# A two-block transformer layer on one core: the planner's price of TensorE's products is changed

## The chip, the cores and the metric

One core of one Trainium2 chip runs the whole program in one launch. The metric is device time in microseconds (us): the median of the timed executions is 954.91 us (three runs, 953.92 to 955.23). Smaller is better.

## The reference, cut to what matters

256 tokens of 1024 features pass through two blocks, all in float32:

```
x = x + gated_branch_mixer(rmsnorm(x))          # w_in (6144 columns), a 31-tap convolution, pooling, w_o
x = x + cross_attention(rmsnorm(x), rmsnorm(mem))
x = x + mixture_of_experts(rmsnorm(x))          # 16 experts, 2 of them for each token
x = rmsnorm(x)                                  # second block:
x = x + rmsnorm(attention_and_scan(rmsnorm(x) @ w_in_2) @ w_out_2)
x = x + rmsnorm(cross_attention_2(rmsnorm(x), rmsnorm(mem_2)))
x = x + rmsnorm(conv_ffn(rmsnorm(x)))           # w_up_2, three-tap convolution, silu * value, w_down_2
```

Every `@ w` is a product with a weight matrix that is read once from the chip's memory, some 178 MB in all.

## The kernel before, in words

**Weights.** All weight matrices lie in one stream, cut into some 330 pieces, nearly all of 512 KB (128 partitions x 1024 floats), in the order of their use. A piece is loaded by SyncE into a tile `stg`. ScalarE (ACT) casts it to `whi`, a float32r tile of fewer bits; VectorE (DVE) writes the remainder `wlo = stg - whi`. An activation is likewise held as two parts, so one block of a weight product is three TensorE (PE) products: whi by the activation's high part, whi by its low part, wlo by its high part. There are six `stg` tiles, four `whi` and three `wlo`, so the splits can be at most two to three pieces ahead of PE.

**Two kinds of work.** A *main line* issues the weight products in the order of the stream (`lin`, `lin_tok`, `lin_both`, `down`, `up_mm`; all products go through `mm`, line 659). Everything else is a *task*: a Python generator that issues a few instructions and yields (class `Task`). Tasks empty PSUM banks, run the norms, the convolution, softmax, routing and the gated scans (`hgrn`, line 1954), and they too issue some products and transposes.

**What sets the order.** All instructions are issued by the Python program once, when the kernel is written, and each engine then runs its own in exactly that order; the order is fixed by hand-written planning and nothing on the chip revises it. The planner keeps a timetable (class `Clock`, line 174): for each engine the time at which it becomes free, and for each tile the time at which its last writer and readers end. `Clock.issue` adds an instruction: it starts when its engine is free and its operands are there, and lasts as long as a price given by the caller. DVE's and ACT's prices are in `Engine.call` (lines 249 to 264), PE's in `mm` (line 662) and in `transpose` (0.107 us, line 666). `now` (line 382) is the time at which the timetable has PE free.

The timetable is read in these places:

- `runnable` (line 420): a task's step that begins with a product may be issued once its operands are there at `now`; another step may be issued if its engine could start it by `now + AHEAD`. AHEAD is 0.8 to 2.6 us by stage (`PACE`, line 281).
- `splits` (line 431): the split of piece n is *due* at `now` plus the sum of `cost(x)` over the pieces from the current one to n (lines 479 to 482). It is put off while its end, by the timetable, lies more than a margin before that. The margin is 0.3 us in a first look and then, after a look at the tasks, 0.5 to 4.0 us by stage (1.0 in the first mixer, 2.0 for the experts, 4.0 in the second mixer, 1.5 in the last stage).
- `block` and `need` (lines 540 and 646): while the main line waits for an activation, due times are moved out by GRACE = 2.0 us.
- `advance` (line 520) ties these together, and is called after every block of weight products until nothing more is due or runnable.

So the prices change no instruction and no operand; they decide how many task steps and splits stand between one weight product and the next, and at which product of the main line a task's own product is put. The prices before are:

```
return nk * nc / 1024 * (1.3 if name.startswith("w_e") else 2.7)
self.c.issue("pe", max(0.107 if slow else 0.027, 0.0022 + n * (4 if slow else 1) / 2400.0), [lhsT, rhs], [out])
```

`n` is the number of columns streamed; `slow` is a float32 product (in norms, attention scores, scans, routing), as against the float32r products of the weights.

Of the kernel before, what the change touches and what calls it, by code (L numbers as in the profile page):

```python
# [35 lines left out]
def weight_plan():  # L36
    """The weight loads in the order of their use: (name, expert, rows, columns)."""
    plan = []
# [87 lines left out]
class Act:  # L126
    """An activation as two float32r parts, with the tasks that write its blocks."""
# [11 lines left out]
class Group:  # L139
    """Two PSUM banks as [128, 4, 256]."""  # L140
# [12 lines left out]
class Task:  # L153
    """A generator that issues instructions; it yields where others may go first."""
# [6 lines left out]
    def at(self):  # L161
        """When its next step can start; None while it waits for others to be issued."""
        t = 0.0 if self.on is None else self.on()
        return None if t is None or self.busy else max(self.ready, t)
# [9 lines left out]
class Clock:  # L174
    """A rough timetable of the engines, kept as the instructions are issued: it decides their order only."""
# [53 lines left out]
class Engine:  # L229
    """An engine whose instructions are entered in the timetable."""  # L230
# [40 lines left out]
class Net:  # L271
# [6 lines left out]
    GRACE = 2.0  # how much later the splits are due while the main line waits for an activation, in us  # L278
    NEAR = 0.5
    # how far the tasks run ahead of the main line, and the slack of the weights' splits, in us  # L280
# [40 lines left out]
    def tile(self, pool, shape, dt, tag, bufs):  # L321
        """A tile of a tag, entered in the timetable as free when the slot's last tile is."""
        t = pool.tile(shape, dt, tag=tag, name=self.name(tag), bufs=bufs)
        name, ring = t.tensor.name, self.rings.setdefault((id(pool), tag), [])
        if len(ring) >= bufs:
            busy = self.busy() if tag == "b" else {x.tensor.name for x in self.kept.get(tag, {}).values()}
            old = min([x for x in ring if x not in busy] or ring, key=self.c.used)
            self.c.born(name, self.c.used(old))
            ring.remove(old)
        ring.append(name)  # L330
        return t

    @contextmanager
    def phase(self, name, **tags):
        """A pool for one part of the program."""
# [26 lines left out]
    def col(self, w, tag="col", bufs=8):  # L362
        """A few columns; those of an own tag at most eight."""
# [45 lines left out]
    def start(self, t):  # L409
        """When the next step of a task would start; None while it waits for others to be issued."""  # L410
# [16 lines left out]
    def wait(*ts):  # L427
        """In a task: yield from it until other tasks are issued."""
        yield None, lambda: max(t.ready for t in ts) if all(t.done for t in ts) else None

    def splits(self, margin=None):
        """Issue the next split of a weight piece, if it can run now; with a margin: if it cannot wait."""
# [20 lines left out]
    def room(self, tag, bufs):  # L453
        """When the next tile of a tag is free."""
# [24 lines left out]
    def cost(self, n):  # L479
        """The time of a piece on TensorE."""  # L480
        name, nk, nc, _ = self.pieces[n]
        return nk * nc / 1024 * (1.3 if name.startswith("w_e") else 2.7)

    def load(self, most=1 << 30):
        """Issue the loads that have a place."""
# [15 lines left out]
    def lend(self, n):  # L501
        """Use free tiles for loads further ahead, until reclaim."""
# [9 lines left out]
    def dma(self, eng, out, in_):  # L512
        """A load of the chip's memory."""
# [6 lines left out]
    def advance(self, goal=None):  # L520
        """Issue one thing beside the main line, if there is one; goal is what the main line waits for."""
# [18 lines left out]
    def need(self, t, until=None):  # L540
        """Issue a task to its end, or until something holds."""
# [18 lines left out]
    def force(self):  # L560
        """Split the next piece though it is late."""
# [7 lines left out]
    def bank(self, n=1):  # L569
        """In a task: a spare PSUM bank, or a list of them, once free; products follow."""  # L570
# [12 lines left out]
    def acquire(self, tag, n, most):  # L583
        """In a task: n of the tiles of a tag that are kept over steps, to be taken off held again."""
# [8 lines left out]
    def busy(self):  # L593
        """The PSUM banks in use."""
# [20 lines left out]
    def gbanks(self, n):  # L615
        """Banks of the main line."""
# [7 lines left out]
    def evac(self, gen, act=None, ks=(), prio=0):  # L624
        """The task that empties the oldest group of the main line without one."""
# [9 lines left out]
    def take(self, name):  # L635
        """The next piece of the plan: a list of (hi, lo) views, one a k block."""
# [9 lines left out]
    def block(self, act, k):  # L646
        """Have a block of an activation issued, and others while it is not there yet."""
# [5 lines left out]
    def settle(self, aps, out):  # L653
        """Let others go while operands of the main line are late."""
# [4 lines left out]
    def mm(self, out, lhsT, rhs, start, stop):  # L659
        n = size(rhs)  # L660
        slow = rhs.dtype == F32
        self.c.issue("pe", max(0.107 if slow else 0.027, 0.0022 + n * (4 if slow else 1) / 2400.0), [lhsT, rhs], [out])
# [6 lines left out]
    def lin(self, name, act, npc=4, nm=4):  # L669
        """One group of up to four output blocks, features on partitions."""  # L670
# [15 lines left out]
    def lin_both(self, name, act, turn):  # L686
        """Two groups of four output blocks, in turns of some input blocks each."""
# [16 lines left out]
    def lin_tok(self, name, act, npc=4):  # L704
        """The two token blocks on partitions, the columns of the loads on the free axis."""
# [40 lines left out]
    def split_gain(self, act, x, gain, k):  # L746
        """act = x * gain for one block, gain a column."""
# [11 lines left out]
    def warm(self, func):  # L759
        """Have the table of a function loaded ahead of its use."""  # L760
# [5 lines left out]
    def seed(self, ms, w, eps=None, out=None):  # L766
        """ScalarE's 1 / sqrt(ms + eps)."""
# [4 lines left out]
    def newton(self, out, ms, w, seed, eps=EPS):  # L772
        """A Newton step from the seed."""
# [5 lines left out]
    def rsqrt(self, out, ms, w):  # L779
        """out = 1 / sqrt(ms + eps)."""  # L780
        self.newton(out, ms, w, self.seed(ms, w))

    class Sum:
        """Sums of squares over blocks that come in pairs: [128, 2, 256] whose total is the sum."""
# [4 lines left out]
        def add(self, x, gain=None, keep=None):  # L789
            """keep: the tag of its tile, as a term of its own."""  # L790
# [19 lines left out]
    def mean_col(self, out, acc, first=False, last=True):  # L810
        """out[:, i] = the mean for the tokens of block i, tokens on partitions."""
# [5 lines left out]
    def rms(self, tiles, r, rc=None):  # L817
        """Task: r = 1/rms on every partition, rc with tokens on partitions."""
# [17 lines left out]
    def memory(self, mem, gname, act, r=None, rc=None):  # L836
        """Tasks: the split of memory * gain, and 1/rms if asked for; the last of them."""
# [39 lines left out]
    def softmax(self, ps, scale, nscale):  # L877
        """Rows of [128, 2, 256] scores to probabilities; scale and its negative are columns, one for each token."""
# [14 lines left out]
    def scales(self, rt, rc, by):  # L893
        """Task: rc * by and its negative."""
# [20 lines left out]
    def xhead(self, h, q, kT, v, out, deps, vdep, sc):  # L915
        """Task: one head of cross attention."""
# [25 lines left out]
    def xattn(self, name, act, rt, rc, kT, v, kdep, vdep, fill):  # L942
        """The heads' outputs, split, features on partitions; fill issues main line work of its own."""
# [52 lines left out]
    def warm_up(self):  # L996
        """Products that nothing reads, while the first loads run: they raise TensorE's clock."""
# [10 lines left out]
    def late_consts(self):  # L1008
        """The constants of the routing and the scans."""
# [232 lines left out]
    def residual(self, name, act, gname, turn=0):  # L1242
        """x += act @ w; the split of x * gain for the next layer and the sum of squares."""
# [36 lines left out]
    def first_max(self, src):  # L1280
        """The maximum over four and the one-hot of its first place."""
# [10 lines left out]
    def route(self, rc, sel):  # L1292
        """Task: for every token its group's one-hot, its place in the group, and (1/rms, four gates)."""
# [63 lines left out]
    def slot_scalars(self, out, bank, sels):  # L1357
        """Of the slots of groups: out[:, g, 0] = 1/rms, out[:, g, 1:5] = 1/rms * gate."""
# [8 lines left out]
    def expert_hidden(self, h, sc, e, ea):  # L1367
        """Task: silu(gate) * up * gate weight of the slots, split, features on partitions; all in the bank of h."""
# [29 lines left out]
    def overflow(self, xh, xl, loads, room):  # L1398
        """The tokens past the first 128 of a group, on the chip only where there are any."""
# [65 lines left out]
    def gather(self, out, xh, xl, sel, k):  # L1465
        """out = the k block of features of the chosen tokens, slots on the free axis."""
# [8 lines left out]
    def moe(self, st, xdone, fill):  # L1475
        """x += the experts' outputs; the banks that hold them."""
# [216 lines left out]
    def between(self, dn):  # L1693
        """x = rmsnorm(x + experts, norm_f_g); the split of x * gains and the scales of the second block's norm."""
# [7 lines left out]
        def first():  # L1702
# [17 lines left out]
            # rsqrt(c / (b + eps) + eps) * rsqrt(b + eps) = rsqrt(c + eps * b + eps * eps)  # L1720
# [36 lines left out]
    def bounds(self):  # L1757
        """Task: the lower bounds of the forget gates, and one minus them."""
# [103 lines left out]
    def gqa(self, qa, ka, vt, deps, sqs, rt, rc):  # L1862
        """Task: normalise and rotate, then a task for each pair of heads."""
# [90 lines left out]
    def hgrn(self, f, kk, qq, q, vt, sg, deps):  # L1954
        """Task: the two gated scans as products over halves of blocks of 2, 4, ... 256 tokens."""
# [15 lines left out]
        def mixed(n, i, h):  # L1971
            """Of q: the left halves of blocks from the backward part, the right ones from the forward part."""
# [21 lines left out]
        def mix(h):  # L1994
            """Of k: the left halves from the forward part, the right ones from the backward part."""
# [5 lines left out]
        def last(t, i, half, g):  # L2001
            """The update for the product of the two token blocks: one half of block i."""
# [10 lines left out]
        def keys():  # L2013
            """Task: of every level the mixed k and the forget products."""
# [19 lines left out]
        def level(n_, h, banks):  # L2034
            """Task: the level's place in the products of all."""
# [75 lines left out]
    def squared(self, st, y, banks, gname):  # L2111
        """Task: the squares of banks of two blocks, the last of them as terms of their own, and y = blocks * gain."""
# [14 lines left out]
    def lin_post(self, name, act, gname, gnext, fill=None, col=False, together=False):  # L2127
        """x += rmsnorm(act @ w, gain); the next layer's split and sum of squares."""
# [48 lines left out]
    def lin_post_tok(self, name, act, gain, gnext):  # L2177
        """The same with the product's tokens on partitions; gain along the free axis."""
# [87 lines left out]
    def down(self, dn, name, ea, first, last=None):  # L2266
        """dn[i][half] += ea @ w, tokens on partitions; with last, it is called as the banks are done."""
# [250 lines left out]
```

## Time and profile before

| what | value |
|---|---|
| median of the timed runs | 954.91 us (953.92 to 955.23) |
| span of the profiled execution, first to last instruction | 954.0 us |
| PE busy | 928.1 us, 97% |
| PE weight loads, beside the products | 856.3 us, 90% |
| DVE busy | 746.7 us, 78% |
| ACT busy | 597.5 us, 63% |
| DMA | 177.72 MB read, 187 GB/s over the span |
| granted PE clock, mean | 0.988 |

For the profiled execution the page gives the span alone as its time; the median of the timed runs is 0.9 us above it. "Busy" is the time in which at least one instruction of the engine was under way. Products are pipelined, so a product's own duration (286 ns for 256 columns) is longer than the distance from its start to the next one's, and it is that distance which counts for throughput.

### The profile page before, as it was taken

What the parts mean: (1) busy time and instruction counts of PE and PEld (TensorE: products, weight loads), DVE (VectorE), ACT (ScalarE), POOL (GpSimd) and SP (SyncE); (2) the same over time, 40 slices, a digit from 0 to 9 for tenths busy, and PEclk for the clock granted to TensorE, in tenths of its full rate; (3) what the DMA queues carried; (4) which work ended last, traced back from release to release, by engine and by line L of the source; (5) the groups of instructions that cost most, each with busy time, mean ns of one, the idle gap of its engine ahead of it and who ended that gap; (6) DMA issues with size and microseconds to landing.
All of it is one profiled execution on the core that took longest, in us unless ns stands there. A gap on an engine that the chain in (4) does not pass through costs nothing.

```text
span 954.0 us, 16266 instructions
## 1 busy us (share of the span) xinstructions
PE 928.1 (97%) x6288; PEld 856.3 (90%) x6288; DVE 746.7 (78%) x1195; ACT 597.5 (63%) x875; POOL 2.5 (0%) x18
## 2 busy tenths in 40 slices
PE   7999999999999998999999999889999899999997
PEld 7999999989989996888888999679998799999995
DVE  5998989767666586998998687969845788888776
ACT  6765444454667647877877579775755666555554
POOL 0000000000000000000000000000000000000000
PEclk8999999999999999999999999899999999999999
DMA  8756746565536728999991536205535456556651
GB/s 285 254 181 194 218 134 213 156 196 180 155 112 198 240 93 307 359 342 353 349 344 65 155 95 204 78 23 165 165 114 183 127 170 206 178 177 177 193 161 45
DMA packets 49910, 179.92 MB, mean 189 GB/s; under 512 B 5664, under 2 KB 5920, under 8 KB 49312
## 3 DMA queue, kind: packets, MB, share of 16 engines
q1 hardware_dynamic: 49824, 178.79, 57.8%
q8 instruction: 52, 0.85, 0.4%
q14 instruction: 34, 0.28, 0.1%
HBM read 177.72 MB, written 1.05 MB: 187 GB/s over the span
## 4 chain that ended last, share of the span: by engine, by line
PE 57%; DVE 3%; ACT 2%; issue 0%; DVEq 0%; ACTq 0%
PE b L663 56%; DVE t L266 2%; ACT t L266 1%; PE b L667 1%; DVE smx L266 0%; ACT prob L266 0%; DVE wlo L266 0%; DVE xT L266 0%; ACT probT L266 0%; DVE prob L266 0%; DVE col L266 0%; ACT whi L266 0%; DVEq L2514 0%; ACT mea L266 0%; DVEq L266 0%
## 5 line engine op out<-in xcount | busy, mean ns | idle before, releaser
L663 PE MATMUL b<-t,whi 128*128 128x256 f32 x2784 | 511.9, 286 | 4.5 <-ACT t L266 3.5
L663 PEld LDWEIGHTS b<-t,whi 128*128 128x128 f32 x2784 | 438.0, 193 | 9.0 <-ACT t L266 4.0
L663 PE MATMUL b<-t,wlo 128*128 128x256 f32 x1392 | 395.4, 284 | 0.0
L266 DVE TENSOR_TENSOR wlo<-stg,whi 128x1024 fp32r<-128x1024 f32 (+1 forms) x269 | 320.9, 1204 | 52.1 <-PE b L663 25.7
L266 ACT CAST whi<-stg 128x1024 fp32r<-128x1024 f32 (+1 forms) x269 | 275.1, 1034 | 120.0 <-PE b L663 84.3
L663 PEld LDWEIGHTS b<-t,wlo 128*128 128x128 f32 x1392 | 268.3, 193 | 0.0
L266 DVE SCALAR_TENSOR_TENSOR t<-pad,vecs,t 128x256 f32<-128x256 f32 x216 | 95.4, 479 | 1.7
L663 PE MATMUL b<-whi,t 128*128 128x512 f32 (+1 forms) x288 | 87.3, 378 | 0.0
L266 DVE TENSOR_TENSOR wlo<-t,whi 128x1024 fp32r<-128x1024 f32 x60 | 71.3, 1219 | 9.0 <-ACT whi L266 3.7
L266 ACT CAST whi<-t 128x1024 fp32r<-128x1024 f32 x60 | 62.8, 1053 | 14.0 <-PE b L663 6.3
L663 PEld LDWEIGHTS b<-whi,t 128*128 128x128 f32 x288 | 52.9, 188 | 8.7
L663 PE MATMUL b<-whi,xgh 128*128 128x512 f32 x128 | 52.5, 410 | 3.5 <-ACTq L1551 3.5
L663 PE MATMUL b<-wlo,t 128*128 128x512 f32 (+1 forms) x144 | 53.8, 373 | 0.2 <-DVE wlo L266 0.2
L266 DVE TENSOR_TENSOR t<-b,t 128x512 fp32r<-128x512 f32 (+1 forms) x38 | 25.6, 687 | 35.7 <-ACT t L266 35.5
L663 PE MATMUL b<-wlo,xgh 128*128 128x512 f32 x128 | 51.2, 400 | 0.0
L663 PE MATMUL b<-whi,xgl 128*128 128x512 f32 x128 | 51.0, 398 | 0.0
L266 ACT ACT_TABLE_LOAD x33 | 42.3, 1283 | 13.5 <-DVE smx L266 7.0
L663 PE MATMUL b<-whi,ea 128*128 128x512 f32 x176 | 50.6, 396 | 0.0
L663 PE MATMUL b<-whi,mea 128*128 128x512 f32 x128 | 42.9, 396 | 0.5 <-ACT mea L266 0.5
L266 ACT ACTIVATE t<-pad,vecs 128x256 f32<-128x256 f32 x52 | 27.7, 587 | 21.4 <-DVE pad L266 21.3
L663 PE MATMUL b<-t,t 128*128 128x128 f32 (+1 forms) x224 | 37.0, 320 | 3.0 <-ACT t L266 1.6
L663 PEld LDWEIGHTS b<-t,t 128*128 128x128 f32 x224 | 32.9, 199 | 6.9 <-ACT t L266 2.5
(218 smaller groups left out, 933.9 us busy)
## 6 DMA issues: line engine op xcount, KB each, us to landing
stg<-wstream SPq DMA_DIRECT2D x259, 512.0 KB, 4.2
t<-wstream SPq DMA_DIRECT2D x60, 512.0 KB, 5.6
t<-memT SPq DMA_DIRECT2D x3, 1024.0 KB, 7.5
stg<-wstream SPq DMA_DIRECT2D x8, 320.0 KB, 2.9
t<-gains SPq DMA_DIRECT2D x1, 1024.0 KB, 7.9
out<-t SPq DMA_DIRECT2D x4, 256.0 KB, 2.0
t<-bands SPq DMA_DIRECT2D x1, 768.0 KB, 5.0
xT<-xT SPq DMA_DIRECT2D x2, 256.0 KB, 6.0
```

The costliest lines, as they stand in the source:

```text
L266: return fn(out, *args, **kw)
L663: self.nc.tensor.matmul(out, lhsT, rhs, start=start, stop=stop, skip_group_check=True)
L667: self.nc.tensor.transpose(out, in_, ident)
```

## The change

Three numbers that the planner uses are replaced. The price of a product in `mm` gets a larger fixed part: 13.5 ns in place of 2.2 ns for float32r, 4 ns for float32, and the least price of a float32 product becomes 222 ns in place of 107 ns. The time of a piece in `cost` follows: 2.88 us in place of 2.7 us, and 1.39 us in place of 1.3 us for the experts' pieces. Docstrings and comments are dropped as well, leaving empty lines in their place; they issue nothing.

```
     def cost(self, n):
         name, nk, nc, _ = self.pieces[n]
-        return nk * nc / 1024 * (1.3 if name.startswith("w_e") else 2.7)
+        return nk * nc / 1024 * (1.39 if name.startswith("w_e") else 2.88)
...
     def mm(self, out, lhsT, rhs, start, stop):
         n = size(rhs)
         slow = rhs.dtype == F32
-        self.c.issue("pe", max(0.107 if slow else 0.027, 0.0022 + n * (4 if slow else 1) / 2400.0), [lhsT, rhs], [out])
+        self.c.issue("pe", max(0.222 if slow else 0.027, (0.004 if slow else 0.0135) + n * (4 if slow else 1) / 2400.0), [lhsT, rhs], [out])
         self.nc.tensor.matmul(out, lhsT, rhs, start=start, stop=stop, skip_group_check=True)
```

By this arithmetic a 256-column float32r product is priced at 120.2 ns in place of 108.9 ns, a 512-column one at 226.8 ns in place of 215.5 ns, a 320-column one at 146.8 ns in place of 135.5 ns, and a float32 product of 128 columns at 222 ns in place of 215.5 ns. The prices of DVE and ACT instructions, the transposes' price, AHEAD, the margins and GRACE stay.

## Rows read from the trace of the kernel before

**Rows 1.** Seven windows that cover the span: us, busy us (count) by engine, PEclk, DMA, GB/s.
```profile
0.00:12.00 12.00, 7.06 (x30) 6.57 (x31) 2.17 (x4) 4.74 (x7) 1.13 (x17) 0.92 0.75 254
12.00:340.00 328.00, 327.45 (x2518) 318.51 (x2516) 260.24 (x432) 190.62 (x269) 1.39 (x1) 0.99 0.60 190
340.00:380.00 40.00, 36.46 (x197) 31.13 (x198) 30.57 (x68) 24.30 (x33) 0.00 (x0) 0.96 0.58 207
380.00:594.00 214.00, 212.73 (x1263) 187.43 (x1262) 180.75 (x236) 162.33 (x220) 0.00 (x0) 1.00 0.72 254
594.00:640.00 46.00, 39.96 (x267) 32.85 (x266) 37.07 (x78) 34.14 (x77) 0.00 (x0) 0.93 0.14 47
640.00:760.00 120.00, 116.62 (x710) 104.42 (x709) 82.21 (x138) 73.72 (x125) 0.00 (x0) 0.99 0.51 154
760.00:955.00 195.00, 187.86 (x1316) 175.34 (x1314) 153.69 (x244) 107.67 (x149) 0.00 (x0) 0.99 0.53 160
```

**Rows 2.** Timeline of PE, 256-column weight products: start us, us, instruction, count.
```profile
99.76 0.28 PE L663 MATMUL b<-t,wlo 128*128 128x256 f32 x1
...
105.74 0.28 PE L663 MATMUL b<-t,wlo 128*128 128x256 f32 x1
...
563.02 0.28 PE L663 MATMUL b<-t,wlo 128*128 128x256 f32 x1
...
572.02 0.28 PE L663 MATMUL b<-t,wlo 128*128 128x256 f32 x1
```

**Rows 3.** The chain that ended last, one expert's products: start us, us, what.
```profile
377.82 8.40 PE b L663 x36
```

**Rows 4.** Timeline of PE, 320-column products of the second mixer, first and last.
```profile
577.11 0.31 PE L663 MATMUL b<-wlo,t 128*128 128x320 f32 x1
...
583.27 0.31 PE L663 MATMUL b<-wlo,t 128*128 128x320 f32 x1
```

**Rows 5.** Groups of PE instructions: busy us, mean ns of one, idle before.
```profile
L663 PE MATMUL b<-wr,xT 128*128 128x20 f32 x32 | 3.9, 256 | 0.0
```

**Rows 6.** Timeline of DVE in the first mixer: convolution steps and splits.
```profile
94.08 1.23 DVE L266 TENSOR_TENSOR wlo<-stg,whi 128x1024 fp32r<-128x1024 f32 x1
95.22 1.67 DVE L266 SCALAR_TENSOR_TENSOR t<-pad,vecs,t 128x256 f32<-128x256 f32 x4
96.96 1.22 DVE L266 TENSOR_TENSOR wlo<-stg,whi 128x1024 fp32r<-128x1024 f32 x1
...
113.44 1.22 DVE L266 TENSOR_TENSOR wlo<-stg,whi 128x1024 fp32r<-128x1024 f32 x1
114.58 1.67 DVE L266 SCALAR_TENSOR_TENSOR t<-pad,vecs,t 128x256 f32<-128x256 f32 x4
116.16 1.22 DVE L266 TENSOR_TENSOR wlo<-stg,whi 128x1024 fp32r<-128x1024 f32 x1
```

**Rows 7.** One window of the first mixer, 60 to 180 us, columns as in rows 1.
```profile
60.00:180.00 120.00, 120.00 (x957) 117.92 (x956) 111.84 (x191) 57.38 (x69) 0.00 (x0) 1.00 0.61 186
```

**Rows 8.** Timeline of DVE, second mixer: instructions that DVE waited before, with the wait.
```profile
576.78 0.83 DVE L266 TENSOR_TENSOR wlo<-stg,whi 128x640 fp32r<-128x640 f32 x1 [0.91 <-PE b L663]
...
579.77 0.17 DVE L266 RECIPROCAL smx<-smx 128x2 f32<-128x2 f32 x1 [1.57 <-ACT prob L266]
...
591.22 0.17 DVE L266 RECIPROCAL smx<-smx 128x2 f32<-128x2 f32 x1 [0.69 <-ACT prob L266]
...
597.51 1.30 DVE L266 TENSOR_TENSOR t<-t,t 128x512 f32<-128x512 f32 x2 [1.02 <-PE b L663]
```

**Rows 9.** The chain that ended last, splits that stand on it: start us, us, what.
```profile
505.95 1.05 ACT whi L266
...
511.06 1.14 DVE wlo L266
...
600.01 1.13 DVE wlo L266
```

**Rows 10.** Timeline of ACT in the second mixer, one of the four table loads from 575 to 602 us.
```profile
580.37 1.28 ACT L266 ACT_TABLE_LOAD   x1
```

More of the change, by code (lines that the diff above doesn't have):

```diff
@@ L481, in cost @@
         name, nk, nc, _ = self.pieces[n]
-        return nk * nc / 1024 * (1.3 if name.startswith("w_e") else 2.7)
+        return nk * nc / 1024 * (1.39 if name.startswith("w_e") else 2.88)
     def load(self, most=1 << 30):
@@ L661, in mm @@
         slow = rhs.dtype == F32
-        self.c.issue("pe", max(0.107 if slow else 0.027, 0.0022 + n * (4 if slow else 1) / 2400.0), [lhsT, rhs], [out])
+        self.c.issue("pe", max(0.222 if slow else 0.027, (0.004 if slow else 0.0135) + n * (4 if slow else 1) / 2400.0), [lhsT, rhs], [out])
         self.nc.tensor.matmul(out, lhsT, rhs, start=start, stop=stop, skip_group_check=True)
```

## The prediction

> **What bounds the kernel now.** I read the windows first, then TensorE's own timeline, then VectorE's beside it, then the chain that ended last.
>
> The windows show where TensorE (PE) is idle [rows 1]. Window length less busy time, in order of time: 4.9, 0.6, 3.5, 1.3, 6.0, 3.4 and 6.2 us (the last window counted to the span's end at 954.0). That is 25.9 us, which is also span less PE busy time, so nothing is missed. For the other 97% PE is fed without a gap. The reader should see that the change, which adds and removes no instruction, can win only what is in these gaps (and a little where the granted clock is under 1, 0.93 of full speed around the biggest gap), but can lose anywhere.
>
> Not all of it is within the planner's reach. The first 4.9 us wait for loads, the 3.5 us stand around the run-time branch after the routing, and the last 6.2 us are the chain after the last product. This leaves 11.3 us: 0.6, 1.3, 6.0 and 3.4. The 6.0 us, between 594 and 640 us, are the gated scans.
>
> **The new prices against the rows.** Every price of the change can be held against a distance between starts.
>
> - 256 columns: from 563.02 to 572.02 there are 25 groups of three products, so 9.00 us / 75 = 120.0 ns. In a faster stretch, 99.76 to 105.74, there are 17 groups: 5.98 / 51 = 117.3 ns [rows 2]. Old price 108.9, new 120.2. The new one is right, or 2.5% high in the faster stretch.
> - 512 columns: one expert is 36 products (24 up, 12 down) in 8.40 us [rows 3], 233 ns each. Old 215.5, new 226.8: still 2.8% low. The new piece price of 1.39 us is six times 232.
> - 320 columns: 14 groups of three in 6.16 us [rows 4], 146.7 ns. Old 135.5, new 146.8.
> - float32: the 16 routing products of 20 columns leave 32 records [rows 5], so one is two passes. The old floor of 107 ns priced one of them.
>
> The Trainium skill speaks against the change: TensorE: Matmul & The Clock Gate, section "Wait — 56ns, not 53.3ns?", gives a warm product columns / 2.4 GHz plus about 2.5 ns, 109 ns for 256 columns, which is the old price. The trace does not agree: 120.0 and 117.3 ns. By the page the new price would be 10% too long and the planner would hand out its splits late, the slower rival below; as the rows contradict it, I give that reading no chance of its own.
>
> So before, the timetable ran PE about 9% too fast. What that did is seen on VectorE (DVE). In the first mixer the planner fills DVE between the weight splits with steps of the 31-tap convolution. A split and four convolution instructions take DVE 2.72 us when nothing holds it (113.44 to 116.16), but at 94.08 to 96.96 the same five take 2.88 us, PE's time for one piece of 24 products [rows 6]: there DVE waits for PE to free a tile. From 60 to 180 us DVE is busy 111.8 of 120 us and PE all 120 [rows 7]. The old price thus left DVE an unplanned cushion of 6 to 7%.
>
> **The change part by part.**
>
> *Direct cost: nothing.* No instruction, transfer or operand changes; the same DMAs go through SyncE's queue in the same order, only the splits that free their tiles may move. If a split moves later its tile's next load does too; with six `stg` tiles that is covered by two to three pieces, 6 to 8 us, outside the experts.
>
> *More task work beside each product.* With PE priced 8 to 10% longer, each weight product carries that much more DVE and ACT work in the order. It matters where the task work is what PE waits for next, in the gated scans. Their inputs are complete at 576.5 us; from then to 594.5 us the main line still has 96 products of 320 columns and 24 of 256. The price of each grows by 11.3 ns: 120 x 11.3 ns = 1.4 us more task work goes in front of the last weight product. It needs room there, and there is some: from 576 to 598 us DVE's four longest waits, each in front of the instruction named, sum to 0.91 + 1.57 + 0.69 + 1.02 = 4.2 us [rows 8]. Bounds: a gain of 0 (the waits only change place) to 4.2 us (all filled). I take 1.4 us, what the price hands out.
>
> *Splits due later.* A piece's price rises by 0.18 us, so a split two pieces ahead is due 0.36 us later and gives way to a task more often. Three splits stand on the chain that ended last, each holding up an instruction that PE waits for: 1.05, 1.14 and 1.13 us [rows 9]. Bounds: 0 to 3.3 us. The shift of 0.18 to 0.36 us is small beside a split's 1.1 us, so I take one of the three, 1.1 us.
>
> *The cushion in the first mixer.* At 2.88 us a piece the planner now fits (2.88 - 1.14) / 0.395 = 4.4 convolution instructions beside a split, where 2.61 us gave 3.7. DVE is then planned full, and on the chip is full: its prices agree with the rows (2.72 us planned and measured for the five). The lead of a split over its product stays at the planned margin of 1.0 us instead of growing. In the fast stretch PE needs 24 x 117.3 ns = 2.82 us a piece, 0.07 us less than planned; over the eight pieces or so around it 0.6 us of the 1.0 us margin goes. Cost 0 as long as the margin holds; up to 3.8 us if not (rival below).
>
> *Tasks' own products.* They are now placed at the first product of the main line at which the timetable has their operands. With all engines priced as measured that is the true moment, give or take a few tenths; before it was safe by 9%. Bounds: -0.5 us (chains shorter) to +1.5 us (a wait of 0.1 to 0.2 us at some ten of them). I take 0.
>
> **Sum.** 1.4 + 1.1 = 2.5 us off the span of 954.0. The profiled execution's span is 0.9 us under the median of the runs shown, and I carry that difference over unchanged: 954.9 - 2.5 = 952.4 us.
>
> **The rivals.**
>
> *Order without effect (34 in 100).* PE busy time stays, the scans are a chain through DVE and ACT whose length no price changes, and the waits only move. For it: 928 of 954 us are PE back to back. Against it: DVE stands idle while the chain is pending [rows 8]. Time: 954.9 us, give or take 1.9.
>
> *The cushion was what fed PE (20 in 100; slower).* Place: the first mixer, pieces with six convolution instructions beside the split. There DVE needs 1.14 + 6 x 0.395 = 3.51 us against PE's 2.88, 0.63 us late. 120 convolution instructions at 4.4 a piece take 27 pieces, of which the planner must give about six such a load (4.4 being a mix of fours and sixes, as a step issues two). If the margin of 1.0 us is already spent when they come, PE waits each time: 6 x 0.63 = 3.8 us, 958.7 us. It decides when the lead of `wlo` over its first product reaches zero. For it: AHEAD and the margins did their work with 9% in hand. Against it: DVE's prices are exact here, so fours and sixes even out over two pieces.
>
> *ACT's table loads fall differently (8 in 100; slower).* In the second mixer ACT alternates between softmax and sigmoid or silu, and each change costs a table load of 1.28 us [rows 10]. A new order that splits a batch adds one or two: 956.2 to 957.5 us. The same could save one, which is in the forecast's low end.
>
> *The forecast (38 in 100).* Faster, 952.4 us; its own range is 954.9 - 7.5 = 947.4 us (both upper bounds) to 953.0.
>
> A version in which the order does not change at all is excluded: due times and `now` are compared at every block.
>
> **How the numbers follow.** The three runs before differ by 1.3 us, and 0.2% (1.9 us) is about what a measurement of this kernel can tell from no change. Faster: the forecast, 0.38. Same: 0.34. Slower: 0.20 + 0.08 = 0.28. Range: from 947.5 us (nearly all of the two gains) to 958.7 us (the cushion's price in full); outside lie a reordering that hits several stages at once, about 1 in 10 at either end. As cases of both signs hold most of the chance, the forecast's own range, 947.4 to 953.0, stands beside it.
>
> **What would show it.** Right: in the profile after, PE's idle time from 594 to 640 us is under 5 us where it was 6.0, DVE's waits between 576 and 598 us sum to about 3 us where the four were 4.2, and one split has left the chain. In the first mixer, five or six convolution instructions stand beside some splits, the convolution ends some 10 us earlier, DVE's busy time from 60 to 160 us rises above 95%, and PE still shows no wait for `wlo`. Wrong: PE waits for `wlo` between 60 and 180 us (the cushion); more than the four table loads that stand between 575 and 602 us now; new short waits of PE for ACT or DVE spread over the attention heads; or the 3.4 us between 640 and 760 us, which I left alone, change.

## The result and the profile after

The kernel after took 963.80 us (median of four runs, 963.25 to 964.25), the kernel before in the same comparison 955.07 (953.92 to 956.64). The ratio is 1.0086, with a 95% interval of 1.0074 to 1.0098: **slower** by 0.86%, clear of its interval, and outside the predicted range of 947.5 to 958.7. The profiled execution took 963.76 us, its span is 961.9, against 954.0 before: 7.9 us to explain.

The page of the kernel after has 16,278 instructions where before had 16,266; products, splits and transfers are the same. So the time went into gaps and the clock. The seven windows, columns as in [rows 1], the last one to the span's end:

```profile
0.00:12.00 12.00, 6.86 (x32) 6.38 (x33) 2.43 (x5) 4.99 (x7) 1.13 (x17) 0.83 0.77 262
12.00:340.00 328.00, 327.62 (x2523) 318.78 (x2523) 263.40 (x467) 192.62 (x272) 1.09 (x1) 1.00 0.60 188
340.00:380.00 40.00, 35.99 (x188) 30.68 (x187) 27.15 (x33) 23.49 (x30) 0.00 (x0) 0.91 0.63 221
380.00:594.00 214.00, 208.15 (x1220) 182.32 (x1219) 178.81 (x236) 157.46 (x217) 0.00 (x0) 0.99 0.70 246
594.00:640.00 46.00, 39.07 (x271) 34.32 (x270) 36.56 (x71) 30.66 (x66) 0.00 (x0) 0.93 0.25 82
640.00:760.00 120.00, 116.13 (x708) 103.09 (x704) 79.41 (x130) 73.17 (x125) 0.00 (x0) 1.00 0.49 150
760.00:962.00 202.00, 195.04 (x1356) 181.79 (x1356) 159.67 (x257) 112.14 (x161) 0.00 (x0) 0.99 0.50 157
```

Up to 380 us no window's idle time moved by more than 0.5 us: the long second window has 0.4 us of idle PE, 0.6 in [rows 1]. The fourth window has 5.85 us of idle PE where [rows 1] has 1.3. Its list of waits points to a place at once. The waits view of the kernel after from 540 to 602 us (who waited for whom: us in total, times, longest) has a pair of lines that the kernel before has nowhere:

```profile
PEld b L663 <- DVE rk L266: 5.0, 1, 5.0
PE b L663 <- DVE rk L266: 4.6, 1, 4.6
```

`rk` holds the rotated keys of the grouped attention (`gqa`, lines 1862 to 1952, in the second mixer). Its chain begins with a product of squares on PE (`b<-sq,cst`), goes through ACT's seed and eight DVE instructions, and ends in the score products (`b<-rk,t`), which are PE's again. PE's timeline in the kernel after, the weight products ahead of it included:

```profile
548.80 0.40 PE L663 MATMUL b<-t,whi 128*128 128x256 f32 x2
...
552.04 0.40 PE L663 MATMUL b<-t,whi 128*128 128x256 f32 x2
...
552.40 0.59 PE L663 MATMUL b<-sq,cst 128*128 128x256 f32 x2
557.59 3.74 PE L663 MATMUL b<-rk,t 64*128 64x256 f32 x16 [4.59 <-DVE rk L266]
```

and the same two steps in the kernel before:

```profile
560.92 0.59 PE L663 MATMUL b<-sq,cst 128*128 128x256 f32 x2
...
572.95 2.10 PE L663 MATMUL b<-rk,t 64*128 64x256 f32 x16
```

Before, 96 weight products (11.5 us) stood between the two; after, none. What PE waits for is plain in DVE's and ACT's timeline of the kernel after: two low parts first, then the chain.

```profile
551.82 2.35 DVE L266 TENSOR_TENSOR wlo<-stg,whi 128x1024 fp32r<-128x1024 f32 x2
...
553.03 0.47 ACT L266 ACTIVATE t<-b,eps 128x256 f32<-128x256 f32 x1 [3.46 <-PE b L663]
...
554.09 0.42 DVE L266 SCALAR_TENSOR_TENSOR t<-b,t 128x256 f32<-128x256 f32 x1
...
557.11 0.42 DVE L266 TENSOR_TENSOR rk<-rk,t 128x256 f32<-128x256 f32 x1
```

The wait is not its whole price. The 16 records of scores took 3.74 us, 2.10 before: PE came out of the wait at half its clock. One-microsecond windows of the kernel after (columns as above; the PEclk column is the third from the end):

```profile
553.00:554.00 1.00, 0.00 (x0) 0.00 (x0) 1.00 (x2) 0.97 (x2) 0.00 (x0) 1.00 0.00 0
558.00:559.00 1.00, 1.00 (x6) 0.79 (x6) 0.13 (x1) 0.63 (x1) 0.00 (x0) 0.50 0.00 0
560.00:561.00 1.00, 1.00 (x8) 0.81 (x4) 0.97 (x3) 0.00 (x0) 0.00 (x0) 0.51 0.00 0
561.00:562.00 1.00, 1.00 (x9) 0.75 (x7) 0.87 (x2) 0.79 (x2) 0.00 (x0) 1.00 0.00 0
```

A granted clock of 0.50 is the lower level, 1.2 GHz. It cost 3.74 - 2.10 = 1.6 us. So the place is worth 4.6 + 1.6 = 6.2 us, and that is what is seen right behind it: the first product of 320 columns starts at 576.52 us before and at 582.94 after, 6.4 us later. PE's timeline, the kernel before and then the kernel after:

```profile
576.52 0.31 PE L663 MATMUL b<-whi,t 128*128 128x320 f32 x1
```
```profile
582.94 0.31 PE L663 MATMUL b<-whi,t 128*128 128x320 f32 x1
```

The remaining 1.5 of the 7.9 us come in the scans: the main line's first product behind them starts at 636.47 us before and at 644.83 after, 8.4 us later, and some 0.5 us of that are made good, in sum, by the end. In the scans PE has a wait of 2.96 us, and half clock behind it; half clock stood in that stage before as well. First the kernel after (PE's timeline, then a window), then the kernel before (a window):

```profile
619.64 2.72 PE L663 MATMUL b<-t,t 128*128 128x128 f32 x11 [2.96 <-DVE t L266]
```
```profile
619.00:626.00 7.00, 6.36 (x28) 5.44 (x28) 5.85 (x13) 5.17 (x11) 0.00 (x0) 0.51 0.00 0
```
```profile
614.00:622.00 8.00, 8.00 (x36) 5.96 (x37) 7.70 (x20) 5.51 (x17) 0.00 (x0) 0.57 0.00 0
```

### The profile page after: what moved, and what is told of

Same layout as the page of the kernel before. It is cut to its first block, busy times and chain, and to the rows that moved or that the text cites. A ratio compares the mean times of both kernels' runs of the same rounds, so it can differ in the third digit from the quotient of the medians.

```text
span 961.9 us, 16278 instructions
## 1 busy us (share of the span) xinstructions
PE 928.9 (97%) x6288; PEld 857.4 (89%) x6288; DVE 747.4 (78%) x1195; ACT 594.5 (62%) x873; POOL 2.2 (0%) x18
## 3 DMA queue, kind: packets, MB, share of 16 engines
HBM read 177.72 MB, written 1.05 MB: 186 GB/s over the span
## 4 chain that ended last, share of the span: by engine, by line
PE 55%; DVE 4%; ACT 2%; issue 1%; DVEq 0%; ACTq 0%
PE b L663 54%; DVE t L266 3%; ACT t L266 1%; PE b L667 1%; DVE wlo L266 1%; DVE xT L266 0%; ACT prob L266 0%; DVE col L266 0%; ACT probT L266 0%; DVE smx L266 0%; ACT whi L266 0%; DVE rk L266 0%; DVEq L2514 0%; DVE ka L266 0%; ACT mea L266 0%
## 5 line engine op out<-in xcount | busy, mean ns | idle before, releaser
L266 DVE TENSOR_TENSOR t<-t,t 128x512 f32<-128x512 f32 (+4 forms) x46 | 29.1, 664 | 17.0 <-ACT t L266 14.0
```

The source lines that it names most:

```text
L266: return fn(out, *args, **kw)
```

## The experiments

Theory A: the score products stand at the wrong place, and the price only brings that out. The task `pair` (line 1868) asks the timetable for a probability tile and for two free PSUM banks, and then issues its products; it never asks when `rk` will be written. Theory B: the first mixer's lost cushion, or low parts split later, slow PE.

**e1: the kernel after, with the question added.**

```
         def pair(b):
+            yield None, lambda: self.c.when([rk[:, 0], rq[:, b]])
             yield from self.acquire("prob", 2, 4)
```

> The changed kernel plus one line: a task of a pair of attention heads asks for its rotated queries and keys (rq, rk) in the timetable before it asks for PSUM banks and issues its score products. Theory A (one product in the wrong place): the changed kernel loses its time because the score products now stand directly behind the step that computes rk and PE waits 4.6 us there, with the granted clock down after it. Then this kernel has no PE wait for rk and takes back 5 to 6 us: 958 us, of the 8.7 us loss some 3 stay for other places. Theory B (the cushion of 9% was what fed PE, loss spread over many places): the guard takes back under 2 us: 962 us or more, as other waits take the place of this one.

Measured: 955.79 us, ratio to before 0.9996 (0.9987 to 1.0006). The one line takes back 8.0 us of the 963.8; by the ratios, 1.0086 and 0.9996, it takes back the whole loss, more than was expected of it. 48 products now stand between the squares and the scores, and the scores wait for nothing. PE's timeline, and the window of the scans, of e1:

```profile
552.26 0.59 PE L663 MATMUL b<-sq,cst 128*128 128x256 f32 x2
...
558.53 2.10 PE L663 MATMUL b<-rk,t 64*128 64x256 f32 x16
```
```profile
594.00:640.00 46.00, 41.11 (x286) 34.65 (x287) 37.50 (x74) 33.91 (x73) 0.00 (x0) 1.00 0.15 53
```

The surplus lies in the scans: from the first product of 320 columns to the main line's first product behind the scans e1 takes 60.32 us (576.72 to 637.04), the kernel after 61.89, the kernel before 59.95. The second fence shows the clock at 1.00 through the scans, where before and after it stood at 0.93. That is not a gain of as much (46 us x 0.07 = 3.2 us): at full clock e1 takes no less time there than the kernel before; the last section shows why. What makes the scans of e1 shorter than those of the kernel after was not taken apart.

**e2 to e4: the parts of the change, each alone in the kernel before**: the price of float32r products (e2), of float32 products (e3), of a piece (e4).

```
-max(0.107 if slow else 0.027, 0.0022 + n * (4 if slow else 1) / 2400.0)
+max(0.107 if slow else 0.027, (0.0022 if slow else 0.0135) + n * (4 if slow else 1) / 2400.0)
```
```
-max(0.107 if slow else 0.027, 0.0022 + n * (4 if slow else 1) / 2400.0)
+max(0.222 if slow else 0.027, (0.004 if slow else 0.0022) + n * (4 if slow else 1) / 2400.0)
```
```
-        return nk * nc / 1024 * (1.3 if name.startswith("w_e") else 2.7)
+        return nk * nc / 1024 * (1.39 if name.startswith("w_e") else 2.88)
```

> The kernel before with the new fixed part of float32r products in mm alone (13.5 ns for 2.2 ns); float32 prices and the piece times in cost as before. Theory A: this part makes PE later in the timetable and lets the score products in front; PE waits about 5 us for rk and the time is 961 to 965 us, as the whole change. Theory B (due dates of splits do it, through cost): 955 to 957 us.

> The kernel before with the new float32 price alone (least price 222 ns for 107 ns, fixed part 4 ns). Theory A: the rk wait does not appear, the time is that of the kernel before within 2 us (953 to 957). Theory B has this part cost little too, since it touches few products: no difference between the theories; a loss over 3 us would refute A's claim that the float32r price alone does it.

> The kernel before with the new piece times in cost alone (2.88 and 1.39 us). Theory A: splits are due 0.18 us later a piece, too little to matter: 954 to 956 us. Theory B (late splits): PE waits for wlo appear and the time is 957 us or more.

Measured: e2 961.89 us, ratio 1.0063 (1.0046 to 1.0080); e3 954.40, 0.9984 (0.9975 to 0.9994); e4 955.67, 1.0000 (0.9990 to 1.0010). The price of the weight products alone brings the wait, at the same place and of the same length, and most of the loss (0.63 of 0.86%); where the rest comes from was not separated. PE's timeline of e2:

```profile
555.47 3.94 PE L663 MATMUL b<-rk,t 64*128 64x256 f32 x16 [4.59 <-DVE rk L266]
```

In e3 the scores start at 571.30 us and in e4 at 571.91, without a wait.

**e5, e6: the question asked 4 us and 2 us too early.** These give the wait in doses (e6 has 2.0 in the place of 4.0).

```
-            yield None, lambda: self.c.when([rk[:, 0], rq[:, b]])
+            yield None, lambda: self.c.when([rk[:, 0], rq[:, b]]) - 4.0
```

> The kernel after with the scores' own readiness asked for, but 4 us too early: the first pair's score products stand 36 TensorE products ahead of their place in the guarded kernel. There they began at 558.5 us and rk was written at 557.4, so with 36 products of 120 ns = 4.3 us less before them TensorE comes to them at 554.2 and waits 3.2 us for rk. Theory A (what is lost is the wait and the half clock that follows a wait of such length: 4.6 us of wait and 3.2 us at granted 0.50 behind it in the kernel after): 3.2 us lost if the clock holds, 4.9 if it falls to 0.50 for as long again: 959.0 to 960.7 beside 955.8 of the guarded kernel. Rival (the loss is in what the moved scores do to all that is ordered behind them, and the wait only goes along with it): the order behind them is not that of the kernel after, so 956 with the wait, or 963 as in the kernel after.

> The same with 2 us: the scores stand 24 products (2.9 us) ahead of their place in the guarded kernel, TensorE comes to them at 555.6 and waits 1.8 us. Theory A: 1.8 us lost, the clock stays at 1.00 after so short a wait: 957.6. Rival (the order behind them): 956 with the wait, or 963.

Measured: e5 961.76 us, ratio 1.0057 (1.0040 to 1.0074); e6 960.55, 1.0043 (1.0028 to 1.0057). The waits came within a tenth of what was worked out (3.17 for 3.2, 1.73 for 1.8), and the clock, in the one execution of each that was profiled, as expected: half after the longer one, full after the shorter. PE's timeline of e5, then its window behind the wait; the same two of e6:

```profile
557.90 3.76 PE L663 MATMUL b<-rk,t 64*128 64x256 f32 x16 [3.17 <-DVE rk L266]
```
```profile
557.00:563.00 6.00, 5.10 (x27) 4.30 (x28) 4.22 (x10) 2.13 (x4) 0.00 (x0) 0.72 0.04 14
```
```profile
558.88 2.10 PE L663 MATMUL b<-rk,t 64*128 64x256 f32 x16 [1.73 <-DVE rk L266]
...
589.92 0.64 PE L663 MATMUL b<-wlo,t 128*128 128x320 f32 x1 [2.84 <-DVE wlo L266]
```
```profile
558.00:562.00 4.00, 3.12 (x25) 2.71 (x26) 3.93 (x9) 0.64 (x2) 0.00 (x0) 1.00 0.31 109
```

But the times are 1 to 3 us over theory A's (959.0 to 960.7, and 957.6). The second row of e6 tells why: 30 us later PE waits 2.84 us for a low part, and e5 has the same wait (2.90 us at 592.10). Neither theory had it. Before that low part, DVE stood at an instruction that waited for ACT, which had a table load in front. ACT's and DVE's timeline of e6, then DVE's of e1:

```profile
583.66 1.28 ACT L266 ACT_TABLE_LOAD   x1
...
586.76 2.36 DVE L266 TENSOR_TENSOR t<-t,t 128x1024 f32<-128x1024 f32 x2 [1.55 <-ACT t L266]
...
589.04 1.55 DVE L266 TENSOR_TENSOR wlo<-stg,whi 128x640 fp32r<-128x640 f32 x2
```
```profile
583.87 1.56 DVE L266 TENSOR_TENSOR wlo<-stg,whi 128x640 fp32r<-128x640 f32 x2 [0.23 <-ACT whi L266]
585.35 2.35 DVE L266 TENSOR_TENSOR t<-t,t 128x1024 f32<-128x1024 f32 x2
```

e1 has a table load there too (at 581.30 us). What differs is the order: in e1 two low parts go ahead of that DVE instruction, in e6 they stand behind it.

So a moved score product costs its wait, at times the clock, and what the other order behind it does. The wait was predictable from rows; the order I could not foresee (e5 and e6 lost by it, e1 did not).

**e7: scores ahead of all other tasks, with the old prices.** The pairs get the first place when they are spawned, until their scores are issued.

```
-        self.pairs = [self.spawn(pair(b), 1) for b in range(4)]
+        self.pairs = [self.spawn(pair(b), -1 if b < 2 else 1) for b in range(4)]
...
+            self.pairs[b].prio = 1
+            self.tasks.sort(key=lambda x: x.prio)
```

> The kernel before with its old prices, but the first two pairs of heads go ahead of all other tasks when they are spawned, until their scores are issued: so the scores stand where the rule puts them in the kernel after, directly behind the step that writes rk, some 25 products (3.0 us) ahead of their place at 572.95 us, i.e. at 570.0. rk was written at 569.74 there. Theory A (with the old prices TensorE runs later than its timetable, which hides that the scores are not asked for their operand): no wait or some tenths, 955 to 956, ratio 1.000. Rival (scores directly behind the step of rk cost 5 us or more in any kernel, and only the choice of place differs): a wait of 3 to 5 us, 959 to 962.

Measured: 955.41 us, ratio 0.9993 (0.9983 to 1.0002), no wait. DVE's timeline of e7, then PE's:

```profile
568.84 0.42 DVE L266 TENSOR_TENSOR rk<-rk,t 128x256 f32<-128x256 f32 x1
```
```profile
560.44 0.59 PE L663 MATMUL b<-sq,cst 128*128 128x256 f32 x2
...
569.59 2.10 PE L663 MATMUL b<-rk,t 64*128 64x256 f32 x16
```

The scores moved forward by 24 products, not as far as the edit was meant to move them. At which weight product the step of `rk` is issued cannot be read from a trace, as it is work of ACT and DVE; but the kernel's program decides it alone and can be run without the chip. Printed from it (places in weight products behind the squares, times of the timetable in us):

| kernel | step of `rk` issued | scores issued | PE's time then | `rk` written |
|---|---|---|---|---|
| before | 36 | 96 | 517.9 | 515.6 |
| e7 | 36 | 72 | 513.1 | 515.6 |
| after | 0 | 0 | 538.9 | 543.7 |
| e1 | 0 | 48 | 544.7 | 543.7 |

So in e7 36 products still stand between the step of `rk` and the scores, and its rival (scores directly behind the step cost 5 us in any kernel) was not tested. But the table sharpens theory A. The kernel after issues the scores while its own timetable has `rk` 4.8 us away; the chip waits 4.59. e7 issues them while its timetable has `rk` 2.5 us away, and the chip waits for nothing: `rk` ends at 569.26 us, 0.3 us before the scores begin, because with the old prices PE reaches a product later on the chip than in the timetable. The distance of 96 products was never planned as a cover. By the code (`start`, `runnable`) the step of `rk`, which begins on ACT, goes out once its start lies within AHEAD of PE's time; at the squares of the kernel before, ACT is booked until 3.5 us after PE's time; in the kernel after it is free.

**e8 to e10: the other place of the same kind.** The products of the scan's levels are issued when the step that writes their keys has been issued, not when it ends.

```
-            yield None, lambda: 0.0 if len(xs) > n_ else None
+            yield None, lambda: self.c.when([xs[n_]]) if len(xs) > n_ else None
```

e8 has both questions, e9 this one alone in the kernel after, e10 this one alone in the kernel before.

> The guarded kernel (955.8) with the same question put to the products of the levels of the gated scan, that are issued as soon as the step that writes their keys is issued, and not when those keys are written. The waits there in the guarded kernel: 0.69 at 604.22, 1.34 at 612.84, 1.82 at 616.98 us. If these products can go behind others, up to 2 to 3 us are gained: 953 to 954. If there is nothing else to issue in that stretch (main line waits for these products itself), nothing: 955.8.

> The kernel after with the question put to the products of the scan's levels alone, not to the scores of the pairs. The 4.6 us wait for rk at 552.99 and the half clock behind it stay. Theory A (two places of the same kind, of which the scores carry the loss): the 2.9 us wait in front of the scan's products at 616.7 us and the 6.2 us at granted 0.50 behind it (3.1 us lost) can go, 963.8 less at most 6.0, and what another wait in the scan's chain takes back: 958 to 962, still over 956. Rival (the scan's products carry the loss, the scores' wait would be made good later): 955 to 957.

> The kernel before, old prices, with the question put to the products of the scan's levels. Theory A (the question is worth something only where the timetable's TensorE is as slow as the real one; with the old prices TensorE's time in the timetable is too early, so that a product asked for when its operand is due there stands later than it must, or where it stood): 955 to 957, no gain. Rival (the question gains in either timetable, as in the guarded kernel, where it went from 955.8 to 954.6): 953.5 to 954.5.

Measured: e8 954.58 us, 0.9985 (0.9975 to 0.9994); e9 959.63, 1.0047 (1.0031 to 1.0062); e10 955.40, 0.9995 (0.9985 to 1.0005). From the 963.8 us of the kernel after, the scores' question takes 8.0 us, the levels' 4.2, both together 9.2 (by the ratios 0.90, 0.39 and 1.01%): less than the sum of the two, so they share a part. In e9 the wait for `rk` stays, and the scans run at full clock. PE's timeline of e9, then its window:

```profile
557.52 3.58 PE L663 MATMUL b<-rk,t 64*128 64x256 f32 x16 [4.59 <-DVE rk L266]
...
618.05 2.05 PE L663 MATMUL b<-t,t 128*128 128x128 f32 x16 [1.17 <-DVE t L266]
```
```profile
617.00:626.00 9.00, 6.31 (x48) 5.29 (x48) 8.89 (x20) 5.86 (x17) 0.00 (x0) 1.00 0.00 0
```

In the kernel before the same question gains nothing that can be measured; but its interval overlaps e8's, so whether it pays only with true prices stays open. e8 is the version with the new prices that stands against both kernels: 9.2 us under the kernel after, 0.15% under before, which is at the edge of what can be told. e3, with the old price of the weight products and no question added, is as far under before (0.16%), so no run shows that it takes the true price of the weight products to get there.

**e11: e8 with a shorter margin for the splits behind the second mixer** (`"post": (2.6, 2.0)` for `(2.6, 4.0)`).

> The kernel after with both questions (954.6 us), and the margin of the weights' splits in the stage behind the second mixer cut from 4.0 to 2.0 us. There a low part's split (1.22 us at 674.39) went ahead of the addition and the splits of the next activation, and TensorE waited 1.04 us at 677.26 for the latter. If the shorter margin lets the activation go first, that wait goes: 953.5 us, ratio to before 0.997 to 0.998. If the split then comes late itself, or another wait takes its place: 954.6 or more.

Measured: 955.35 us, 0.9990 (0.9981 to 0.9999). A miss: the wait of e8 (1.04 us at 677.26) stayed, as PE's timeline of e11 shows.

```profile
679.65 0.39 PE L663 MATMUL b<-t,whi 128*128 128x256 f32 x1 [1.05 <-DVE t L266]
```

## Why the prediction was wrong

**The step that failed** is *Tasks' own products*: "They are now placed at the first product of the main line at which the timetable has their operands. With all engines priced as measured that is the true moment, give or take a few tenths", cost 0, at most 1.5 us. The first sentence is untrue of this code, and so is the line on `runnable` ahead of the prediction ("once its operands are there"). A task's products are placed where the task *asks*, and `pair` asks for banks, not for `rk`; a product's start is worked out only when it has already been issued. With true prices the timetable can see PE waiting and still do it (the table at e7: 4.8 us). One such place cost 6.2 us, four times the bound, and a second one (the levels) sits in the scans. The bound was worked out as many small errors of price (a wait of 0.1 to 0.2 us at ten places); one missing question has no such size. The prediction had read "before it was safe by 9%" correctly and did not follow it to the lines where that safety was all there was.

**Direct cost nothing**: right.

**The new prices are right**: confirmed, which makes the result instructive. In PE's timeline of the kernel after, in the section on the result, 27 weight products take 552.04 - 548.80 = 3.24 us, 120.0 ns each, as in [rows 2]. An estimate from the fixed part that the Trainium skill gives (TensorE: Matmul & The Clock Gate, section "Wait — 56ns, not 53.3ns?") is 109 ns, which would make the new price too long; this trace, too, does not agree. Nor is the loss of the kind that a price too long would bring: PE waits for no late low part in the kernel after.

**The cushion in the first mixer**, cost 0, and its rival: the cost was right, and the rival is refuted. The convolution ends at 148.0 us where it ended at 177.9 (30 us earlier; "some 10" was said), DVE is busy for 96.4 of the 100 us from 60 to 160 (93.1 before), and no line of PE's waits names `wlo` in the whole kernel after. e1 has the same first mixer and costs nothing. That DVE waited for PE there before was an inference: the waits view of before from 60 to 180 us has DVE waiting for ACT (4.3 us in its longest line) and nowhere for PE.

```profile
60.00:160.00 100.00, 100.00 (x779) 97.46 (x778) 96.44 (x173) 48.27 (x59) 0.00 (x0) 1.00 0.60 182
```

**More task work beside each product**, 1.4 us gained in the scans: not shown. In the kernel after, PE's idle time from 594 to 640 us rose, from 6.0 to 46.00 - 39.07 = 6.9 us, where under 5 was to show the gain. In e1 it is 46.00 - 41.11 = 4.9 us, but between the two products of the main line named at e1 the stage took 60.32 us, 59.95 before: the shorter idle time did not shorten it. The 24 products of 256 columns that were counted up to 594.5 us run from 597.2 to 600.3.

**Splits due later**, 1.1 us gained: not gained. e4, which has this part alone, gives 1.0000 (0.9990 to 1.0010). The term was too large from the start: the first two of the three splits in [rows 9] lie where PE has no wait over 0.5 us, and PE's idle time from 380 to 594 us is 1.3 us in all. The chain that ended last has eight lines of splits in the kernel after, where [rows 9] has three. Two of the eight answer to the first two of those; the other six are new, three of them ahead of `rk` and three behind the second mixer, where PE then waited 1.05 us at 687.47 for an activation that DVE wrote behind a split. That wait stands in e1 too, and neither in e2 nor in e4: it needs more of the change than one of these two parts, and which was not taken apart.

**Table loads**: the rival is refuted; the page of after counts 31 loads, 33 before. As a way in which an order can turn against PE it came up in e6.

**Order without effect**, 34 in 100: without the one place, this is what the change is. e1 gives 0.9996 (0.9987 to 1.0006), which no change would give too.

## What to carry to other kernels

Where a hand-made order works although its prices are wrong, look for what the wrong prices protect: every instruction that is issued without asking when its operands are ready lives on the slack that the error leaves, and loses it when the price is corrected. Before a planner's prices are corrected, list its waits by operand and check that each product of a side task asks for what it reads; put the missing questions in first (in e1 one line was worth 8 us), then change the price. A wait of PE for an operand that nothing planned for can cost more than its length, where the clock falls behind it and the slowed products are what the rest waits for; the section below shows both cases.

## What the runs showed of the hardware

The clock made some waits dearer than they look. After waits of 4.6 and 3.2 us (after, e5) PE ran the scores at a granted 0.50, 3.74 and 3.76 us for 16 records; after 1.7 us (e6) at 1.00, 2.10 us.

The length of the wait just ahead does not settle it alone, and half clock does not always cost time. In the scans the kernel before and e7 issue the same products in the same order and have the same three waits up to one point (1.56, 0.47 and 1.21 us). Behind it the kernel before stood at a granted 0.57 for 8 us (its window is in the section on the result), e7 at 1.00. Yet the next 16 records of scan products start 9.33 us behind that point before and 9.27 us in e7 (613.93 to 623.26 and 613.28 to 622.55): at full clock PE is done sooner and waits for ACT and DVE instead. PE's timeline of the kernel before; PE's timeline of e7, then its window:

```profile
613.93 2.72 PE L663 MATMUL b<-rk,t 64*128 64x256 f32 x8 [1.21 <-DVE t L266]
...
623.26 2.02 PE L663 MATMUL b<-t,t 128*128 128x128 f32 x16 [0.60 <-DVE t L266]
```
```profile
613.28 1.78 PE L663 MATMUL b<-rk,t 64*128 64x256 f32 x8 [1.21 <-DVE t L266]
...
619.13 1.16 PE L663 MATMUL b<-t,t 128*128 128x128 f32 x8 [1.52 <-ACT prob L266]
...
622.55 2.02 PE L663 MATMUL b<-t,t 128*128 128x128 f32 x16 [1.39 <-DVE t L266]
```
```profile
613.30:621.30 8.00, 6.29 (x40) 4.80 (x40) 7.70 (x20) 5.51 (x18) 0.00 (x0) 1.00 0.00 0
```

In the kernel after it is otherwise: the 16 records behind the wait of 2.96 us stand on the chain that ended last, with 3.80 us at half clock where 16 such records take 2.05 in e9 at full clock. That is 1.75 us there, out of 6.4 us of busy PE at half clock. No price in the planner knows of any of this.
